# Two transformer blocks on one core: the modulations' closing products come one chunk later

## The chip, the cores and the metric

The kernel runs on one NeuronCore of a Trainium2 chip, as one launch. The metric is device microseconds (us) for the whole launch, lower is better. The engines are named as the profile names them: PE is TensorE's products, PEld its weight loads, DVE is VectorE, ACT ScalarE, POOL GpSimd, and SP is SyncE, whose queue issues nearly all transfers.

## What is computed

Two blocks of two layers each act on 512 tokens of width 1024. In the first block each layer mixes by sliding-window attention, retention and gated linear attention; in the second a layer has attention and a gated feed-forward part, and there is a second stream of 256 context tokens. Every layer is modulated: a vector `c` (one for the tokens, one more for the context) is multiplied by a large weight matrix, and the result is split into shifts, scales and gates.

```
mod = c_act @ w_mod + b_mod                                # 1024 x 3072 in block 1, 1024 x 6144 in block 2
shift, scale, gate = jnp.split(mod[:, None, :], 3, axis=-1)
h = rms_norm(x, pre_gain) * (1.0 + scale) + shift
...
return x + gate * rms_norm(y, post_gain)
```

These matrix-vector products are what the change is about. They don't depend on the tokens, so that they can be made at any time before their layer needs them.

## The kernel before

The work is written as Python generators which are woven into one another; a scheduler then fixes one order of instructions for each engine, and each engine runs its own in that order. Nearly all matrix work is in `dense` (line 427): 1024 x 128 weights arrive by a transfer into a tile `wr`, ACT rounds them to `wh` (line 422), POOL or DVE makes the rest `wl` (lines 398, 400), and PE adds 24 products into a PSUM bank: 16 with `wh`, 8 with `wl`. PSUM has eight banks; the kernel uses two under the name `b`, two under `d`, and two pairs under `s`. Everything short goes through the two banks `b`: scores of the linear attention, transposes, sums of squares, and the modulations.

The modulations are a background stream: `mods` (line 729) is a generator, and `tick` (line 360) advances it at a given rate while a stage is woven. It is started with lists of groups: once in layer 0 of block 1 (three calls of `mods` in a chain: 4, 12 and 8 chunks), once in layer 1 of block 1 (4 chunks), once from the context stage on (12), and once in the feed-forward part of block 2's first layer (24). A chunk is 256 columns of the weights and goes like this:

- Two transfers (line 738) bring the 1024 x 256 weights as two tiles `mr`, out of three buffers.
- `mod_sum` (line 708) makes 8 products `b<-mr,mc`. The vectors `mc` are only 32 columns wide, so that four products, for four quarters of the rows, stand in four strips of 32 partitions of one bank `b`; the other four add to them. In the trace each product is two instructions.
- `mod_cols` (line 719) copies that bank on ACT into a tile `ms` (line 723), and two small products with the constant `mod_sel` (`b<-mod_sel,ms`) add the four strips and turn the result into columns, in another tile of the name `b`.
- DVE adds the bias and writes the columns where they are wanted (line 744).

In the start of the kernel (line 634 on) four larger chunks are made in the same way by the same two functions, without the background. Which of the two banks a `b` tile gets is the scheduler's choice.

Of the kernel before, what the change touches and what calls it, by code (L numbers as in the profile page):

```python
# [11 lines left out]
F32 = mybir.dt.float32  # L12
# [11 lines left out]
KD = D // 128  # L24
# [102 lines left out]
def _consts():  # L127
# [5 lines left out]
    for l in range(7):  # L133
        s = 1 << l
        qt = (i // s) % 2 == 1
        start = (i // s) * s
        w[:, l] = np.where(qt, (j >= start) & (j <= i), (j > i) & (j < start + s))
        masks[:, l] = (j // (2 * s) == i // (2 * s)) & ((j // s) % 2 == 0) & ((i // s) % 2 == 1)
# [61 lines left out]
class Net:  # L200
# [187 lines left out]
    def mm(self, out, lhsT, rhs, start, stop):  # L388
        self.nc.tensor.matmul(out, lhsT, rhs, start=start, stop=stop)  # L389
# [244 lines left out]
    def start(self):  # L634

        nc, I = self.nc, self.I
        with self.phase("start") as ph:
            x = ph.tile([128, KD, S], F32, name=self.name("x"))
            for i in range(8):
                w = slice(KD // 8 * i, KD // 8 * (i + 1))  # L640
                nc.sync.dma_start(x[:, w], I["x"][:, w])
            self.setup()
            outs, b, vecs = self.mod1[0]
            m = outs[0]
            r = self.rstd(self.square_sums([x[:, k, :] for k in range(KD)], S), S)
            gain = self.common.tile([128, KD], F32, name="gain_start")
            h = self.new_h(S)
            acc = [self.bank([128, S], "d") for _ in range(2)]
            for _ in range(2):
                w = self.wide()  # L650
                acc += [w[:, 0, :], w[:, 1, :]]
            ws = []
            units = 0, 1, 11, 12, 13, 14
            for c in range(4):
                pieces = []
                for p in range(4):
                    raw = self.tl(ph, [128, 2, 512], F32, "raw", 6)
                    nc.sync.dma_start(raw, I["w_mod_start"][c, :, 2 * p:2 * p + 2, :])
                    pieces.append(raw)
                ps = self.mod_cols(self.mod_sum(pieces, vecs, range(4)), ph)  # L660
                for i, g in enumerate((1, 0)):
                    w = slice(g * KD + 2 * c, g * KD + 2 * c + 2)
                    nc.vector.tensor_add(m[:, w], ps[:, 2 * i:2 * i + 2, 0], b[:, w])
                if c < 3:
                    for u in units[2 * c:2 * c + 2]:
                        src = I["w_in"][0, u].rearrange("p k c -> p (k c)")
                        ws.append(self.weights(src, 1024, (ph, f"u{u}") if u else None))
                ks = slice(2 * c, 2 * c + 2)
                nc.vector.scalar_tensor_tensor(gain[:, ks], m[:, KD + 2 * c:KD + 2 * c + 2], 1.0, self.pre[:, 0, ks],
                                               op0=ALU.add, op1=ALU.mult)  # L670
                for k in (2 * c, 2 * c + 1):
                    self.norm_tile(h, x, k, S, r, gain, m[:, 0:KD])
                if c:
                    self.outer(ws[:2 * c], h, acc, range(2 * c, 2 * c + 2))
                if c < 3:
                    self.outer(ws[2 * c:], h, acc[2 * c:], range(2 * c + 2))
            with self.ahead(-50):
                self.angles()
        return h, dict(zip(units, acc))
# [36 lines left out]
            self.mm(ps[j:j + 32, :], c[:, k, :], pieces[k // per][:, k % per, :], x < 4, x >= 4)  # L716
        return ps

    def mod_cols(self, ps, pool):

        n = ps.shape[1]
        t = self.tl(pool, [128, n], F32, "ms", 1)
        self.nc.scalar.copy(t, ps)
        o = self.bank([128, n // 128, 2])
        for f in range(n // 128):
            self.mm(o[:, f, :], t[:, f * 128:f * 128 + 128], self.mod_sel, f == 0, f == n // 128 - 1)
        return o

    def mods(self, m, wsrc, groups):
        nc = self.nc  # L730
        outs, b, vecs = m
        for g in groups:
            for q in range(4):
                pieces = []
                for p in range(2):
                    raw = self.tl(self.mp, [128, 4, 256], F32, "mr", 3)
                    yield
                    nc.sync.dma_start(raw, wsrc[4 * g + q, :, 4 * p:4 * p + 4, :])
                    pieces.append(raw)
                o = self.mod_cols(self.mod_sum(pieces, vecs, (1, 0)), self.mp)  # L740
                w = slice(g * KD + 2 * q, g * KD + 2 * q + 2)
                for i, (_, n) in enumerate(vecs):
                    if g < n:
                        nc.vector.tensor_add(outs[i][:, w], o[:, :, i], b[:, w])

    def gain1(self, gain, scale, name):

# [1208 lines left out]
```

## Time and profile before

| | us |
|---|---|
| median of 3 runs | 2879.4 |
| lowest, highest | 2874.68, 2889.54 |
| the profiled execution | 2882.13 |
| its span, from the first to the last instruction | 2880.3 |
| PE busy in it | 2473.7 |
| DVE, ACT, POOL busy | 1267.5, 1187.0, 1077.7 |

The profile is of one execution; its span leaves out 1.8 us that lie around the first and the last instruction. An engine's idle time is put down to the engine or transfer whose signal came last before it went on. The mean clock that TensorE was granted is 0.91 of its full speed.

### The profile page before, as it was taken

To read this page: it belongs to the slowest core of one execution; us is meant where nothing else is said; L and a number is where in the kernel's file an instruction comes from. 1 tells how busy PE (TensorE), PEld (TensorE's weight loads), DVE (VectorE), ACT (ScalarE), POOL (GpSimd) and SP (SyncE) were. 2 spreads that over 40 slices of the span, in tenths; PEclk is the share of its full clock that TensorE was granted. 3 is DMA by queue.
4 is the path that set the end of the run, shared out by engine and by line. 5 is a ranking of instruction groups with operands and counts; after the bars stand their busy time and mean duration, and the time that the engine had idled before them with its cause. 6 is when DMAs were issued, how large, how long until landed. Compare 5 with 4: busy or idle time off the path is not lost. (4 is left out here: it accounts for less than half of the span.)

```text
span 2880.3 us, 35460 instructions
## 1 busy us (share of the span) xinstructions
PE 2473.7 (86%) x13052; PEld 2008.7 (70%) x13052; DVE 1267.5 (44%) x2065; ACT 1187.0 (41%) x2227; POOL 1077.7 (37%) x754
## 2 busy tenths in 40 slices
PE   6887888677979987669999899999878969799997
PEld 4765566566657765548998777777766757588886
DVE  3645356335646644356453631222635647421212
ACT  2533355333537534346554422222434536333222
POOL 2434325334623551123455632323541221433334
PEclk9988889788989987779999999999888979899999
DMA  7454544435344553335653544453442254333332
GB/s 239 131 189 143 182 132 160 139 111 169 108 128 138 188 188 119 117 107 139 178 161 136 172 145 162 146 183 115 160 135 96 86 159 114 113 110 97 101 95 74
DMA packets 170817, 400.58 MB, mean 139 GB/s; under 512 B 19378, under 2 KB 60820, under 8 KB 167316
## 3 DMA queue, kind: packets, MB, share of 16 engines
q1 hardware_dynamic: 170644, 398.31, 42.6%
q8 instruction: 104, 1.70, 0.2%
q14 instruction: 69, 0.57, 0.1%
HBM read 339.85 MB, written 58.39 MB: 138 GB/s over the span
## 5 line engine op out<-in xcount | busy, mean ns | idle before, releaser
L398 POOL TENSOR_TENSOR wl<-wr,wh 128x1024 fp32r<-128x1024 f32 (+3 forms) x245 | 537.0, 2193 | 890.8 <-ACT wh L422 435.5
L422 ACT CAST wh<-wr 128x1024 fp32r<-128x1024 f32 (+3 forms) x367 | 353.4, 963 | 745.8 <-PE d L389 290.1
L389 PE MATMUL d<-hh,wh 128*128 128x512 f32 x960 | 405.6, 422 | 20.3 <-ACT hh L556 7.8
L389 PE MATMUL d<-hl,wh 128*128 128x512 f32 x960 | 399.1, 416 | 3.3 <-POOL hl L398 1.4
L389 PE MATMUL d<-hh,wl 128*128 128x512 f32 x960 | 261.8, 402 | 0.0
L400 DVE SCALAR_TENSOR_TENSOR wl<-wr,wh 128x1024 fp32r<-128x1024 f32 (+3 forms) x122 | 151.5, 1242 | 226.5 <-PE d L389 96.3
L389 PEld LDWEIGHTS d<-hh,wh 128*128 128x128 f32 x960 | 192.4, 200 | 72.1 <-issue 12.1
L389 PEld LDWEIGHTS d<-hl,wh 128*128 128x128 f32 x960 | 192.0, 200 | 45.9 <-issue 4.9
L389 PEld LDWEIGHTS d<-hh,wl 128*128 128x128 f32 x960 | 184.7, 194 | 40.6 <-issue 2.5
L921 POOL TENSOR_TENSOR oy<-pg,pg 64x256 f32<-64x256 f32 (+1 forms) x72 | 57.4, 797 | 299.9 <-DVE pg L919 95.6
L400 DVE SCALAR_TENSOR_TENSOR pg<-b,pg 128x512 fp32r<-128x512 f32 (+1 forms) x208 | 137.3, 666 | 67.7 <-ACT pg L404 66.1
L389 PE MATMUL b<-hh,wh 128*128 128x512 f32 x416 | 165.2, 397 | 0.0
L389 PE MATMUL b<-hl,wh 128*128 128x512 f32 x416 | 164.0, 394 | 0.0
L404 ACT CAST pg<-b 128x512 fp32r<-128x512 f32 (+1 forms) x208 | 117.3, 571 | 88.9 <-PE b L896 83.4
L869 DVE TENSOR_REDUCE sm<-s 128x1 f32<-128x768 f32 (+3 forms) x144 | 121.1, 847 | 65.0 <-PE s L389 64.2
L389 PE MATMUL d<-hc,wh 128*128 128x256 f32 x656 | 104.4, 309 | 24.9 <-DVE rp L400 12.5
L937 DVE SCALAR_TENSOR_TENSOR rp<-rp,d 128x512 f32<-128x512 f32 (+1 forms) x77 | 46.8, 607 | 165.0 <-ACT rp L936 164.9
L389 PE MATMUL d<-hid,wh 128*128 128x512 f32 (+1 forms) x528 | 117.6, 365 | 1.9 <-POOL hid L398 1.5
L1725 DVE SCALAR_TENSOR_TENSOR rp<-rp,b 128x512 f32<-128x512 f32 (+1 forms) x64 | 38.1, 595 | 175.8 <-PE b L389 175.3
L389 PEld LDWEIGHTS d<-hc,wh 128*128 128x128 f32 x656 | 94.0, 209 | 30.2 <-ACT wh L422 12.1
L389 PE MATMUL b<-hid,wh 128*128 128x512 f32 (+1 forms) x528 | 110.4, 360 | 0.0
L389 PEld LDWEIGHTS d<-hid,wh 128*128 128x128 f32 x528 | 90.1, 191 | 21.2 <-issue 2.9
(412 smaller groups left out, 5191.3 us busy)
## 6 DMA issues: line engine op xcount, KB each, us to landing
wr<-in_ffn_w_in SPq DMA_DIRECT2D x132, 512.0 KB
mr<-in_ada_w SPq DMA_DIRECT2D x96, 512.0 KB
wr<-in_ffn_w_out SPq DMA_DIRECT2D x48, 512.0 KB
x<-x SPq DMA_DIRECT2D x20, 1024.0 KB
wr<-in_w_in SPq DMA_DIRECT2D x38, 512.0 KB
mr<-in_w_mod SPq DMA_DIRECT2D x32, 512.0 KB
wr<-in_ev_w_in SPq DMA_DIRECT2D x20, 512.0 KB
wr<-in_ffn_w_out SPq DMA_DIRECT2D x24, 384.0 KB
```

Source lines behind the costliest of these rows:

```text
L389: self.nc.tensor.matmul(out, lhsT, rhs, start=start, stop=stop)
L398: self.nc.gpsimd.tensor_sub(out, src, hi)
L400: self.nc.vector.scalar_tensor_tensor(out, src, scale, hi, op0=ALU.mult, op1=ALU.subtract)
L404: self.nc.scalar.copy(hi, src)
L422: nc.scalar.copy(hi[:, :n], raw[:, :n])
L869: nc.vector.reduce_max(c, s, axis=AX.X, negate=True)
L921: nc.gpsimd.tensor_tensor(d, sel(t), sel(rs), op=ALU.mult)
L937: nc.vector.scalar_tensor_tensor(t, t, 1.0, ps, op0=ALU.add, op1=ALU.mult)
L1725: nc.vector.scalar_tensor_tensor(g, g, 0.5, pu, op0=ALU.mult, op1=ALU.mult)
```

## The change

`mod_cols` is taken apart: `mod_take` copies the bank on ACT into `ms`, and `mod_cols` makes the small products from a copy. In the start the two follow each other as before. In `mods`, a chunk now makes its sums and its copy, and then the small products and the bias additions of the chunk before; `ms` has two buffers instead of one. A call's first chunk has no small products behind it, and its last chunk's come after one more `yield`, a step of the background later.

```diff
--- before.py
+++ after.py
@@ -657,7 +657,7 @@
                     raw = self.tl(ph, [128, 2, 512], F32, "raw", 6)
                     nc.sync.dma_start(raw, I["w_mod_start"][c, :, 2 * p:2 * p + 2, :])
                     pieces.append(raw)
-                ps = self.mod_cols(self.mod_sum(pieces, vecs, range(4)), ph)
+                ps = self.mod_cols(self.mod_take(self.mod_sum(pieces, vecs, range(4)), ph, 1))
                 for i, g in enumerate((1, 0)):
                     w = slice(g * KD + 2 * c, g * KD + 2 * c + 2)
                     nc.vector.tensor_add(m[:, w], ps[:, 2 * i:2 * i + 2, 0], b[:, w])
@@ -716,11 +716,14 @@
             self.mm(ps[j:j + 32, :], c[:, k, :], pieces[k // per][:, k % per, :], x < 4, x >= 4)
         return ps
 
-    def mod_cols(self, ps, pool):
-
-        n = ps.shape[1]
-        t = self.tl(pool, [128, n], F32, "ms", 1)
+    def mod_take(self, ps, pool, bufs):
+        t = self.tl(pool, [128, ps.shape[1]], F32, "ms", bufs)
         self.nc.scalar.copy(t, ps)
+        return t
+
+    def mod_cols(self, t):
+
+        n = t.shape[1]
         o = self.bank([128, n // 128, 2])
         for f in range(n // 128):
             self.mm(o[:, f, :], t[:, f * 128:f * 128 + 128], self.mod_sel, f == 0, f == n // 128 - 1)
@@ -729,6 +732,15 @@
     def mods(self, m, wsrc, groups):
         nc = self.nc
         outs, b, vecs = m
+
+        def finish(t, g, q):
+            o = self.mod_cols(t)
+            w = slice(g * KD + 2 * q, g * KD + 2 * q + 2)
+            for i, (_, n) in enumerate(vecs):
+                if g < n:
+                    nc.vector.tensor_add(outs[i][:, w], o[:, :, i], b[:, w])
+
+        last = None
         for g in groups:
             for q in range(4):
                 pieces = []
@@ -737,11 +749,12 @@
                     yield
                     nc.sync.dma_start(raw, wsrc[4 * g + q, :, 4 * p:4 * p + 4, :])
                     pieces.append(raw)
-                o = self.mod_cols(self.mod_sum(pieces, vecs, (1, 0)), self.mp)
-                w = slice(g * KD + 2 * q, g * KD + 2 * q + 2)
-                for i, (_, n) in enumerate(vecs):
-                    if g < n:
-                        nc.vector.tensor_add(outs[i][:, w], o[:, :, i], b[:, w])
+                t = self.mod_take(self.mod_sum(pieces, vecs, (1, 0)), self.mp, 2)
+                if last is not None:
+                    finish(*last)
+                last = t, g, q
+        yield
+        finish(*last)
 
     def gain1(self, gain, scale, name):
```

The scheduler makes a new order from this. Three places of PE's order follow; in the names, `mr` are the modulation weights, `mc` the vectors, `hh` and `hl` the two parts of the activations, `qb` and `pg` the operands of the linear attention.

Layer 1 of block 1, the first of its four chunks; before:

```order
L389 MATMUL d_5315<-hh_4171,wh_5311 128x512
L389 MATMUL b_5288<-mr_5106,mc_529 32x256 x4
L389 MATMUL b_5288<-mr_4979,mc_529 32x256 x4
L389 MATMUL d_5315<-hl_4172,wh_5311 128x512
L389 MATMUL d_5315<-hh_4171,wh_5311 128x512
L389 MATMUL d_5315<-hl_4172,wh_5311 128x512
L389 MATMUL b_5299<-mod_sel,ms_5297 128x2 x2
L389 MATMUL d_5315<-hh_4171,wh_5311 128x512
```

The same place now, and then the second chunk:

```order
L389 MATMUL d_5310<-hh_4171,wh_5306 128x512
L389 MATMUL b_5288<-mr_5106,mc_529 32x256 x4
L389 MATMUL b_5288<-mr_4979,mc_529 32x256 x4
L389 MATMUL d_5310<-hl_4172,wh_5306 128x512
L389 MATMUL d_5310<-hh_4171,wh_5306 128x512
L389 MATMUL d_5310<-hl_4172,wh_5306 128x512
```

```order
L389 MATMUL b_5437<-mr_5376,mc_529 32x256 x4
L389 MATMUL b_5437<-mr_5299,mc_529 32x256 x4
L389 MATMUL b_5431<-qb_1077_4845,pg_5354 128x512
L389 MATMUL d_5460<-hh_4171,wh_5456 128x512
L389 MATMUL d_5460<-hl_4172,wh_5456 128x512
L389 MATMUL b_5448<-mod_sel,ms_5297 128x2 x2
L389 MATMUL d_5460<-hh_4171,wh_5456 128x512
```

The first chunk's small products are gone from behind its sums; they stand in the second chunk (`ms_5297` is the first chunk's copy), again some products behind its sums.

Latent projections and windowed attention of block 2, the last chunk but one; before:

```order
L498 MATMUL b_10559<-ident,sm_10340 128x128 x2
L389 MATMUL d_10500<-pg_10551,ev_9910 128x512
L389 MATMUL b_10569<-mr_10297,mc_529 32x256 x4
L389 MATMUL b_10569<-mr_10033,mc_529 32x256 x4
L389 MATMUL b_10580<-mod_sel,ms_10578 128x2
L896 MATMUL b_10587<-ident,ep_10463 128x128
L896 MATMUL b_10587<-ident,ep_10473 128x128
L896 MATMUL b_10587<-ident,ep_10483 128x128
L896 MATMUL b_10587<-ident,ep_10493 128x128
L389 MATMUL b_10580<-mod_sel,ms_10578 128x2
L896 MATMUL b_10598<-ident,ep_10463 128x128
```

Now:

```order
L498 MATMUL b_10554<-ident,sm_10335 128x128 x2
L389 MATMUL d_10495<-pg_10546,ev_9905 128x512
L389 MATMUL b_10564<-mr_10292,mc_529 32x256 x4
L389 MATMUL b_10564<-mr_10028,mc_529 32x256 x4
L389 MATMUL b_10575<-mod_sel,ms_10021 128x2 x2
L909 MATMUL b_10582<-ident,ep_10458 128x128
L909 MATMUL b_10582<-ident,ep_10468 128x128
L909 MATMUL b_10582<-ident,ep_10478 128x128
L909 MATMUL b_10582<-ident,ep_10488 128x128
L909 MATMUL b_10593<-ident,ep_10458 128x128
```

The transposes of `ep` stand behind the small products as before; these are now of the chunk before (`ms_10021`), and both of them stand ahead of the transposes.

The feed-forward part of block 2, one of 24 chunks; before:

```order
L389 MATMUL b_15061<-hh_14290,wl_15058 128x512 x8
L389 MATMUL b_15095<-mr_15093,mc_529 32x256 x4
L389 MATMUL b_15095<-mr_15023,mc_529 32x256 x4
L389 MATMUL d_15118<-hh_14290,wh_15114 128x512
L389 MATMUL d_15118<-hl_14291,wh_15114 128x512
L389 MATMUL d_15118<-hh_14290,wh_15114 128x512
L389 MATMUL d_15118<-hl_14291,wh_15114 128x512
L389 MATMUL b_15106<-mod_sel,ms_15104 128x2 x2
L389 MATMUL d_15118<-hh_14290,wh_15114 128x512
```

Now:

```order
L389 MATMUL b_15056<-hh_14290,wl_15053 128x512 x8
L389 MATMUL b_15090<-mr_15088,mc_529 32x256 x4
L389 MATMUL b_15090<-mr_15018,mc_529 32x256 x4
L389 MATMUL b_15101<-mod_sel,ms_15011 128x2 x2
L389 MATMUL d_15113<-hh_14290,wh_15109 128x512
L389 MATMUL d_15113<-hl_14291,wh_15109 128x512
```

The small products have moved from behind four products of the next unit to the place right behind the sums, and read the copy of an earlier chunk. In SP's order some transfers of `mr` have changed places with transfers near them; the first such change is behind the weights `wr` that line 417 issues at 159.56 us of the trace.

## Rows read from the trace of the kernel before

**Rows 1.** Page, part 1: busy time, share of the span, instructions of each engine.
```profile
PE 2473.7 (86%) x13052; PEld 2008.7 (70%) x13052; DVE 1267.5 (44%) x2065; ACT 1187.0 (41%) x2227; POOL 1077.7 (37%) x754
```

**Rows 2.** TensorE's waits (total us, times, longest): whole run, then 0 to 130 us.
```profile
PE b L389 <- ACT ms L723: 36.8, 15, 15.8
...
PE b L389 <- ACT ms L723: 2.1, 3, 0.7
```

**Rows 3.** Timeline, 128 to 150 us: start, length, engine, line, operation [idle before <-releaser].
```profile
141.62 0.36 ACT L723 COPY ms<-b 128x256 f32<-128x256 f32 x1
...
142.04 1.01 PE L389 MATMUL b<-mod_sel,ms 128*128 128x2 f32 x4 [3.83 <-ACT ms L723]
```

**Rows 4.** Timeline, 148 to 172 us, SyncE, ScalarE and TensorE.
```profile
159.56 10.38 SPq L417 DMA_DIRECT2D wr<-in_w_in  x4
...
166.11 1.04 ACT L422 CAST wh<-wr 128x1024 fp32r<-128x1024 f32 x1 [11.74 <-DMA wr<-in_w_in]
...
167.21 0.50 PE L389 MATMUL d<-hh,wh 128*128 128x512 f32 x1 [3.88 <-ACT wh L422]
```

**Rows 5.** Timeline, 189 to 226 us, TensorE, SyncE and VectorE.
```profile
204.70 1.07 PE L389 MATMUL b<-mr,mc 128*32 128x256 f32 x16 [0.96 <-DVE oy L1122]
...
206.02 4.08 SPq L738 DMA_DIRECT2D mr<-in_w_mod  x2
...
208.23 0.73 DVE L1122 COPY_PREDICATED oy<-gla_mask,b 128x512 f32<-128x512 uint8 x1
...
208.79 0.88 PE L389 MATMUL b<-mod_sel,ms 128*128 128x2 f32 x4 [2.13 <-ACT ms L723]
...
219.10 1.88 PE L389 MATMUL b<-mr,mc 128*32 128x256 f32 x16 [2.47 <-DMA mr<-in_w_mod]
```

**Rows 6.** Timeline, 664 to 700 us, TensorE, ScalarE and VectorE.
```profile
666.87 0.39 PE L389 MATMUL d<-hl,wh 128*128 128x512 f32 x1
...
670.76 1.04 ACT L422 CAST wh<-wr 128x1024 fp32r<-128x1024 f32 x1 [7.20 <-DMA wr<-in_w_in]
...
674.52 1.01 PE L389 MATMUL b<-mod_sel,ms 128*128 128x2 f32 x4 [7.26 <-ACT ms L723]
...
675.40 0.77 PE L389 MATMUL d<-hh,wh 128*128 128x512 f32 x1
...
675.97 0.63 PE L389 MATMUL d<-hl,wh 128*128 128x512 f32 x1
...
676.16 0.87 DVE L400 SCALAR_TENSOR_TENSOR qb<-pg,qb 32x256 fp32r<-32x256 f32 x2
...
676.40 0.63 PE L389 MATMUL d<-hh,wh 128*128 128x512 f32 x1
...
682.23 1.56 PE L389 MATMUL b<-qb,pg 128*128 128x512 f32 x6
```

**Rows 7.** Timeline, 1250 to 1285 us, ScalarE and TensorE.
```profile
1267.98 0.42 ACT L503 ACTIVATE rp<-xc 128x256 f32<-128x256 f32 x1 [4.92 <-DMA eqnm<-rp]
...
1269.02 0.58 ACT L918 COPY pg<-b 64x512 f32<-64x512 f32 x1
...
1269.92 0.59 PE L389 MATMUL b<-mod_sel,ms 128*128 128x2 f32 x2 [15.83 <-ACT ms L723]
...
1270.37 1.09 PE L896 MATMUL b<-ident,ep 128*128 128x128 f32 x4
```

**Rows 8.** Timeline, 1720 to 1750 us, TensorE and its weight loads (PEld).
```profile
1723.13 1.07 PE L389 MATMUL b<-mr,mc 128*32 128x256 f32 x16
...
1724.13 0.19 PEld L389 LDWEIGHTS d<-hh,wh 128*128 128x128 f32 x1 [0.41 <-issue]
...
1724.47 0.40 PE L389 MATMUL d<-hl,wh 128*128 128x512 f32 x1
...
1724.71 0.40 PE L389 MATMUL d<-hh,wh 128*128 128x512 f32 x1
...
1725.18 0.50 PE L389 MATMUL b<-mod_sel,ms 128*128 128x2 f32 x4
```

## The prediction

> **What bounds the kernel now.** I read the page's busy times first: TensorE is busy 2473.7 us, 86% of the span, and no other engine is above 44% [rows 1]. So a gain has to come out of TensorE's idle time, some 406.6 us (2880.3 − 2473.7), or out of products that cost less. The change touches one kind of idle time, the small products' wait for ScalarE's copy `ms`, and the waits by releaser show how much that is: 36.8 us in 15 waits, of which 2.1 us in 3 belong to the start, whose order stays [rows 2]. That leaves 34.7 us in 12 waits, 1.2% of the time: no gain out of this wait can be larger.
>
> Then I looked those 12 up in the timeline. Four are long: 3.83 us at 142 [rows 3], 2.13 at 209 [rows 5], 7.26 at 675 [rows 6] and 15.83 at 1270 [rows 7]. The first three are first chunks of a call of `mods`, which lose the small products behind their sums. The other eight share 34.7 − 29.05 = 5.65 us. In the feed-forward part, with 24 of the 64 chunks, the small products start without a wait [rows 8]. For each long wait the question is what TensorE meets next: a wait that goes is worth only what the next one doesn't take back.
>
> **The change, part by part.** The count of products, copies, additions and transfers stays; what moves is the place of the small products, and with it some transfers in SP's order. I work against the profiled execution, 2882.13 us, 2.7 above the median of 2879.4.
>
> *The wait at 142, 3.83 us.* ScalarE casts the weights `wh` at 166.11 after 11.74 us of waiting for a transfer `wr` that SP issued at 159.56, and TensorE's product behind that waits 3.88 us and starts at 167.21 [rows 4]. SP's order is the old one up to that issue, so the transfer comes no earlier, and TensorE would wait 3.8 us more at 167 in place of 142. I take 0; the ends are 0 and −3.8.
>
> *The wait at 209, 2.13 us.* The next stop is at 219.10, 2.47 us for a transfer `mr` [rows 5]. Its issue at 206.02 needs a buffer that the sums at 204.70 set free, not the small products; so it lands as before and takes the gain back. I take 0 (0 to −2.1).
>
> *The wait at 675, 7.26 us.* Here the late part starts in earnest: the products behind it are `d<-hh,wh` and its kin, whose cast ended at 671.8 (670.76 + 1.04), long before [rows 6]. So the stall as such goes. Two things decide what is left. Behind the stall, products follow each other at 0.43 us (676.40 − 675.97), against 0.24 in the feed-forward part (1724.71 − 1724.47) [rows 6, 8]; 20 of them fill 675.40 to 682.23, that is 0.34 each, and at 0.24 they would take 4.8 in place of 6.8, 2.0 us less. With this, the upper end is 7.3 + 2.0 = 9.3. But the next user, `b<-qb,pg` at 682.23, needs the splits `qb`, which VectorE finishes at 677.03 (676.16 + 0.87) whatever TensorE does, since ScalarE ahead of them was held by the transfer `wr` for 7.20 us [rows 6]. So that product can come forward by at most 682.23 − 677.03 = 5.2. I take −5, the nearer bound (0 to −9.3).
>
> *The wait at 1270, 15.83 us.* This is the largest and the one that I don't count. ScalarE reaches the copy late because it waits 4.92 us for the transfer `eqnm`, until 1267.98, and ends its copy out of a `b` bank only at 1269.60 (1269.02 + 0.58) [rows 7]. In the new order the small products read an old copy, but they and the transposes `b<-ident,ep` behind them need two `b` banks: one is that which ScalarE empties at 1269.60, the other holds the new sums until the held copy is made. So the name of the wait changes, from the copy to a bank, and its end moves from 1269.92 to about 1269.6. I take −0.3 (0 to −15.8).
>
> *The eight small waits, 5.65 us.* The two `b` banks decide here too: where the small products' bank is the one that this chunk's own sums have filled, they still wait for the same copy. I take about a third, −2 (0 to −5.7).
>
> *The seam in the feed-forward part.* After the sums, the first product lies 0.34 us ahead of the next (1724.47 − 1724.13), an ordinary one 0.24, so that the seam costs 0.10 [rows 8]. Before, the small products made a second break in the run of `d`; now they stand at the seam, and 24 × 0.10 = 2.4 us can go at most. I take the half, −1.2 (0 to −2.4).
>
> By the Trainium skill, page "TensorE: Matmul & The Clock Gate", Part 2 ("What happens when you issue a matmul"), TensorE pulls weight loads ahead of products that still run. The row speaks against it at this place: the weight load behind the sums stands idle for 0.41 us with nothing to wait for [rows 8]. By the rule the seam would vanish with the change, and this term would be −2.4.
>
> *What it adds.* One more step of the background per call of `mods` costs no engine time. A second `ms` buffer costs 1 KB per partition. The swapped places in SP's queue, from 160 us on through layer 0: a transfer put behind a pair of `mr` comes up to 4.08 us later [rows 5], the `mr` as much earlier. I take 0 with ends −4 and +4, since both kinds were waited for at some place [rows 4, 5].
>
> The sum: 0 + 0 − 5 − 0.3 − 2 − 1.2 = −8.5. From 2882.13 this gives 2873.6 for a profiled execution and 2870.9 for the median; I say **2871**. With the terms' ends around it, without the 15.83, this case reaches from 2862 to 2879.
>
> **The rivals.**
>
> *More comes back (2860).* The gaps at 142 and 209 aren't taken back, since a unit ahead in time pulls later issues forward, and the clock behind 675 recovers: −3.8 − 2.1 − 9.3 − 2 − 2.4 = −19.6. For it: every releaser behind those waits is a chain through the other engines, and SP's issues follow buffers that TensorE sets free. Against it: both transfers were issued by events that the change leaves in place [rows 4, 5].
>
> *Nothing comes back (2879).* The −5 at 675 and the rest are taken by the next transfer or the next user of a bank. For it: ScalarE itself sits 7.20 us in wait of `wr` there [rows 6], so the stretch may go at the pace of the transfers; and TensorE's small waits are all for two banks. Against it: the products right behind the stall had their operands ready. The Trainium skill, same page, section "HAM oscillation — how this bites in real kernels", reports that double-buffered PSUM results gave a kernel that already ran well no further gain (126.6 to 125.5 us); by that this case would be the likeliest, and only rows of the feed-forward part, where nothing waits [rows 8], agree with it so far.
>
> *Slower (2896): the late product waits for a bank's reader on VectorE.* Before, the small products came after their own copy, some products behind the sums. Now they can stand right behind the sums, where the other `b` bank may still be under its reader. The nearest case: sums ending at 205.77 (204.70 + 1.07), and the copy with mask on VectorE, which reads a `b` bank behind the splits, ending at 208.96 (208.23 + 0.73) [rows 5]: 3.2 us, with all of TensorE's queue behind it. The 24 chunks of layer 0 stand beside such work; if 8 of them pay it, that is 25.5 − 8.5 = 17 us more. It decides from a reader that ends over 1.07 us behind the start of the sums, and from 8 chunks on it outweighs 14.4 + 8.5. For it: the sums themselves wait 0.96 us for this reader [rows 5]. Against it: in the new order, too, several products stand between sums and small products at nearly all places of that stretch.
>
> **How the numbers follow.** The forecast has 0.49, more coming back 0.21, nothing 0.21, slower 0.09. The range, 2856 to 2888, takes in the forecast's own, the first two rivals with 4 us below the first for part of the 15.83, and 9 above the second for a few bank waits or swapped transfers; outside are the third rival and most of a full return of the 15.83. About 0.5%, 14.4 us, is what a measurement of this kernel can tell from no change: faster means below 2865.0, slower above 2893.8. Faster: the first rival and 0.02 of the forecast's lower end, 0.23. Slower: the third, 0.09. Within: 0.68.
>
> **What the profile of the changed kernel would show.** Right: TensorE's wait for `ms` falls from 36.8 us to under 8; the gap near 675 is gone and `b<-qb,pg` behind it comes some 5 us earlier against its neighbours; near 167 the wait for `wh` grows to about 7.7, near 219 that for `mr` to about 4.6; near 1270 a wait of some 15 us stays, now put down to a bank's reader on ScalarE; in the feed-forward part TensorE stays busy throughout, with a pitch per chunk shorter by 0.05. Wrong: if the 15.83 us at 1270 vanish without a wait of that size within the next 50 us; if `b<-mod_sel,ms` or the sums wait for VectorE in layer 0 for over 10 us in all; or if the feed-forward stretch moves by over 3 us, which no term here allows.

## The result: 1.1% faster, more than the range allowed

| | us |
|---|---|
| before, median of 4 runs | 2877.9 |
| changed, median of 4 runs (2843.78 to 2853.33) | 2847.62 |
| ratio, 95% interval | 0.9889 (0.9855 to 0.9924) |
| changed, 6 more runs beside 11 of before | 2849.07 against 2878.02, ratio 0.9896 (0.9875 to 0.9917) |
| the profiled execution of the changed kernel | 2850.94, span 2849.2 |

The forecast was 2871 with a range down to 2856. The change takes 30 us, 3.5 times the 8.5 that I had summed up.

TensorE's busy time on the page and its waits over the whole run now read:

```profile
PE 2467.3 (87%) x13052; PEld 2004.1 (70%) x13052; DVE 1262.4 (44%) x2065; ACT 1187.1 (42%) x2227; POOL 1079.5 (38%) x754
```

```profile
PE b L389 <- DVE oy L1135: 19.0, 10, 4.2
...
PE d L389 <- ACT wh L422: 17.7, 4, 6.3
...
PE b L389 <- ACT pg L931: 16.4, 2, 16.0
...
PE b L389 <- DMA mr<-in_w_mod: 7.1, 3, 3.8
...
PE b L389 <- ACT ms L721: 4.5, 5, 1.6
```

The wait for `ms` has fallen from 36.8 to 4.5 us [rows 2], as was meant. A reader could stop here and call that the gain. The other rows forbid it: 16.0 us stand under another name now, the wait for a cast `wh` and that for VectorE's `oy` have grown. So I set the same products of both traces (the n-th of a name) against each other and read how far the changed kernel is ahead: 0.2 us at 110, 24.7 at the end of layer 0 (470 to 480 us of before), 22.3 at 620, 23.9 at 770, 24.5 at 1350, 25.4 at 1640, 26.3 at 1970, 31.6 at the end. **Most of the gain is made between 130 and 460 us**, where I had expected none to stay. (The 5.3 us behind 1970, where no modulation is left, belong to that execution of before: all sixteen kernels of the next section run 1.1 to 7.7 us ahead of it from 1970 to 2270.)

Place by place, the rows that answer to those of before. At 142 the wait is gone, and the clock with it is better; TensorE in 128 to 150 us, before:

```profile
128.00:150.00 22.00, 18.17 (x82) 14.32 (x81) 12.95 (x18) 7.26 (x15) 12.90 (x13) 0.84 0.40 139
```

and changed (the first number after the 22.00 is TensorE's busy time, the third last the granted clock):

```profile
128.00:150.00 22.00, 22.00 (x108) 17.02 (x107) 15.12 (x22) 9.09 (x19) 13.78 (x14) 1.00 0.43 148
```

The next stop takes a part back, in the changed kernel's timeline at 158 to 168 us:

```profile
162.71 1.04 ACT L422 CAST wh<-wr 128x1024 fp32r<-128x1024 f32 x1 [13.84 <-DMA wr<-in_w_in]
...
163.81 0.80 PE L389 MATMUL d<-hh,wh 128*128 128x512 f32 x1 [5.98 <-ACT wh L422]
```

5.98 in place of 3.88 us [rows 4]. The transfer is not where it was, though: the cast starts at 162.71, not 166.11.

Around 675 the stall is gone and three others stand there, in the changed kernel at 640 to 700 us:

```profile
652.04 2.79 PE L389 MATMUL b<-qb,pg 128*128 128x512 f32 x6 [2.54 <-DVE oy L1135]
...
659.06 1.86 PE L389 MATMUL b<-rq,rk 128*128 128x512 f32 x4 [4.23 <-DVE oy L1135]
...
665.08 0.47 PE L389 MATMUL d<-pg,rv 128*128 128x512 f32 x1 [2.37 <-DMA rv<-rv]
```

The product `b<-qb,pg` of 682.23 [rows 6] now starts at 652.04, 30.2 us earlier and so 7.9 ahead of its neighbours' 22.3; by 700 all but 1.6 of that is gone.

At 1270 the wait has only changed its name, in the changed kernel at 1222 to 1250 us:

```profile
1242.05 0.42 ACT L503 ACTIVATE rp<-xc 128x256 f32<-128x256 f32 x1 [4.96 <-DMA eqnm<-rp]
...
1243.10 0.58 ACT L931 COPY pg<-b 64x512 f32<-64x512 f32 x1
...
1243.73 1.01 PE L389 MATMUL b<-mod_sel,ms 128*128 128x2 f32 x4 [16.02 <-ACT pg L931]
```

The same squares, the same transfer, the same reader of a `b` bank as in [rows 7], and 16.02 us in place of 15.83. In the feed-forward part a chunk of the changed kernel reads:

```profile
1697.11 1.07 PE L389 MATMUL b<-mr,mc 128*32 128x256 f32 x16
1698.11 0.61 PE L389 MATMUL b<-mod_sel,ms 128*128 128x2 f32 x4
1698.58 0.48 PE L389 MATMUL d<-hh,wh 128*128 128x512 f32 x1
1698.89 0.40 PE L389 MATMUL d<-hl,wh 128*128 128x512 f32 x1
```

From the start of the sums to the second product behind them that is 1.78 us with the small products inside. Before, the same piece took 1.34 (1724.47 − 1723.13), and the small products with the next product 0.45 more than a plain product's 0.23 [rows 8]: 1.79. There is next to nothing in it.

### The profile page after: what moved, and what is told of

It reads as the page before. It is cut to its first block, busy times and chain, and to the rows that moved or that the text cites. A ratio compares the mean times of both kernels' runs of the same rounds, so it can differ in the third digit from the quotient of the medians.

```text
span 2849.2 us, 35397 instructions
## 1 busy us (share of the span) xinstructions
PE 2467.3 (87%) x13052; PEld 2004.1 (70%) x13052; DVE 1262.4 (44%) x2065; ACT 1187.1 (42%) x2227; POOL 1079.5 (38%) x754
## 5 line engine op out<-in xcount | busy, mean ns | idle before, releaser
L389 PE MATMUL d<-hh,wh 128*128 128x512 f32 x960 | 399.1, 416 | 19.3 <-ACT hh L556 7.8
L389 PE MATMUL b<-hh,wl 128*128 128x512 f32 x416 | 104.0, 390 | 0.0
```

## Experiments

e1 to e8 and e12 to e15 keep the changed kernel's code and switch its two parts call by call (e9 to e11 are the kernel before with one line more, e16 is the changed kernel): `late` (the small products come a chunk late) and `tail` (the extra step at a call's end).

```diff
-    def mods(self, m, wsrc, groups):
+    def mods(self, m, wsrc, groups, late=True, tail=True, bufs=2):
...
+                if not late:
+                    finish(t, g, q)
+                    continue
                 if last is not None:
                     finish(*last)
                 last = t, g, q
-        yield
-        finish(*last)
+        if tail:
+            yield
+        if last is not None:
+            finish(*last)
```

With both off in all calls, every engine's order is that of the kernel before. The table gives all runs; "fetch 3" and "fetch 4" are the starts of the first transfer `rk` of the retention's third and fourth head in layer 0, "held" the time that SP waited ahead of fetch 3 (from 225 us on) by the profile's waits put down to a transfer `mr`, blank where its longest such wait was under 3.5 us, "end" the start of the first `b<-blk,rp` behind 420 us, just after layer 0's windowed attention. These four are from one profiled execution each; executions differ by up to 3 us from the start on.

| kernel | median | ratio, 95% interval | fetch 3 | held | fetch 4 | end |
|---|---|---|---|---|---|---|
| before | 2878 to 2880 | | 259.3 | 8.4 | 313.9 | 460.3 |
| changed | 2847.6 | 0.9889 (0.9855 to 0.9924) | 243.9 | | 295.2 | 434.6 |
| e1 late and step, layer 0 only | 2853.5 | 0.9899 (0.9883 to 0.9915) | 243.9 | | 296.2 | 437.5 |
| e2 all but layer 0 | 2871.3 | 0.9966 (0.9951 to 0.9980) | 259.0 | 8.3 | 312.6 | 457.4 |
| e3 step alone | 2866.8 | 0.9943 (0.9926 to 0.9961) | 243.1 | | 302.7 | 438.4 |
| e4 late, first call, no step | 2881.0 | 1.0000 (0.9987 to 1.0013) | 252.6 | 8.4 | 307.4 | 454.1 |
| e5 late, no step | 2875.1 | 0.9982 (0.9968 to 0.9996) | 256.2 | 8.4 | 310.4 | 450.2 |
| e6 before, rate 0.73 | 2865.4 | 0.9953 (0.9939 to 0.9968) | 247.7 | | 299.0 | 438.9 |
| e7 before, rate 0.79 | 2865.2 | 0.9952 (0.9937 to 0.9968) | 252.8 | | 303.9 | 445.7 |
| e8 changed, rate 0.70 | 2858.1 | 0.9930 (0.9909 to 0.9951) | 243.5 | | 300.2 | 438.1 |
| e9 pause at the fifth chunk | 2869.5 | 0.9962 (0.9947 to 0.9978) | 244.6 | | 295.9 | 441.7 |
| e10 pause at the sixth chunk | 2876.3 | 0.9986 (0.9972 to 1.0000) | 253.0 | 8.3 | 300.0 | 444.9 |
| e11 pause at the ninth chunk | 2879.8 | 1.0003 (0.9988 to 1.0018) | 258.8 | 8.3 | 313.1 | 451.7 |
| e12 late and step in layer 0, rate 0.79 | 2874.2 | 0.9990 (0.9982 to 0.9999) | 243.0 | | 310.3 | 448.5 |
| e13 step, late in calls 1 and 3 | 2859.2 | 0.9938 (0.9916 to 0.9961) | 246.4 | | 306.5 | 436.1 |
| e14 step, late in call 2 | 2861.1 | 0.9935 (0.9912 to 0.9957) | 241.7 | | 292.7 | 429.5 |
| e15 step alone, late in the other 40 | 2859.9 | 0.9928 (0.9908 to 0.9948) | 240.5 | | 302.8 | 436.9 |
| e16 changed, again | 2849.1 | 0.9896 (0.9875 to 0.9917) | 242.7 | | 295.1 | 430.2 |

Below, gains are differences of medians to before in the same rounds (2879.8 for e1 to e4, 2877.9 for e5 to e12, 2878.0 for e13 to e16).

**Which stretch, which part.** e1 has `late=False, tail=False` in the three calls outside layer 0, e2 in the three calls of layer 0; e3 has `late=False` in layer 0 (the step stays) and the others off; e4 is late in the first call only, without the step:

```diff
-self.mods(m1[0], I["w_mod"][0], (2,))
+self.mods(m1[0], I["w_mod"][0], (2,), tail=False)
```

> Late only in the 24 chunks of layer 0 of block 1; the other 40 chunks as before. The engines' orders are those of the changed kernel up to the end of layer 0 and those of the kernel before behind it. In the traces the same products of both kernels lie 21 to 23 us apart at the end of that stretch. Theory A (the gain is made in layer 0 and kept): 22 to 26 us less than before. Theory B (my prediction's picture: layer 0 takes its own gains back, the sum comes from the later places): 0 to 5 us less.

> The complement: the 24 chunks of layer 0 as before, late in the other 40. Theory A: 3 to 8 us less than before (some 1.5 near 675, a little in the feed-forward part). Theory B: the larger part of the 30 us, 20 or more. If the two parts don't interact, the gains of this run and of the one with layer 0 alone add up to that of the change.

> Nothing is late; only the one more step of the background at the end of each of the three calls in layer 0 is kept (and the second copy buffer). It moves later chunks and with them 586 rows of TensorE's order and the places of some transfers. Theory C (the gain of layer 0 comes from the order that the scheduler happened to make): 12 to 25 us less than before. Theory D (it comes from the small products that no longer wait for the copy): within 4 us of before.

> Late only in the first call of mods (4 chunks, from 130 to about 190 us), without the extra step, so that only 36 rows of TensorE's order differ from before and 6 of SP's. It takes away the wait of 3.83 us at 142 alone. My prediction: 0 (the transfer behind it takes it back). Theory D: 3 to 6 us less, since in the changed kernel TensorE's clock there is 1.00 in place of 0.84 and the weights behind it land 3.4 us earlier. Theory C: 0 to 3 us less.

Layer 0 alone is worth 26.3, the rest 8.5; together that is 34.8, some 5 more than the change itself, which the intervals allow. Theory A holds: most of the gain is made in layer 0. But e3, in which nothing is late, already has 13.0 of it, and its TensorE still waits 38.8 us in all for `ms`. And e4, without the 3.83 us at 142, is the kernel before to within 0.13% (3.7 us): its profile shows the same clock of 1.00 there and then 6.52 us of waiting for `wh`. So about half of what pays in layer 0 is not what the change is about; the extra step moves the background, and with it the order.

**Late without the step, and the order moved by other means.** e5 has `tail=False` in layer 0 and the rest off; e6 and e7 are the kernel before with another rate, e8 the changed kernel with another rate:

```diff
-                                       self.mods(ada[0], I["ada_w"][0], (1, 0))), 0.76)
+                                       self.mods(ada[0], I["ada_w"][0], (1, 0))), 0.73)
```

> Late in the 24 chunks of layer 0, but without the extra step at the end of the three calls (there the last chunk's small products come at once). Theory H (the gain of layer 0 comes through SP's queue: a transfer mr whose buffer is still in use holds up the fetches rq, rk, rv of the retention behind it; what counts is how many mr stand ahead of the third and fourth fetch): here these are 20 and 29 of 48, as in the kernel before (19 and 28 in the changed one and with the step alone), so 0 to 6 us less than before. Theory D (the small products that no longer wait): 15 to 26 us less.

> The kernel before with one number changed: the background of layer 0 advances at 0.73 in place of 0.76 per step. Nothing is late and nothing else moves by hand. 19 and 28 mr stand ahead of the third and fourth retention fetch. Theory H: 10 to 20 us less than before, as with the step alone. Theory D: within 4 us of before.

> The kernel before with the rate 0.79: 21 and 30 mr stand ahead of these fetches, one more than before. Theory H: 5 to 20 us more than before. Theory D: within 4 us of before. If both this and the run with 0.73 are faster, the order of before was simply an unlucky one among many.

> The changed kernel in full with the rate 0.70: 17 and 25 mr ahead of these fetches. Theory H: 5 to 15 us less than the changed kernel (35 to 45 less than before), as long as the chunks that are left at the end of the layer find room beside the windowed attention. Theory D: the same as the changed kernel, 30 less than before.

Theory D falls with e5: 2.8 us by medians, 1 to 9 by the interval, with 21 of layer 0's 24 chunks late. Theory H in its first form, a count of `mr` ahead of the fetches, falls with e7: one more `mr` ahead, and yet 12.7 us faster; the changed kernel with 0.70 was some 10 us slower than with 0.76, where 5 to 15 less were expected. What holds is that the order counts: 0.73 and 0.79 are both 12 to 13 us faster than 0.76 with nothing else changed. The kernel before had an order that its neighbours don't have.

**What is bad in that order.** The traces show one place. SP's queue in the kernel before, 225 to 262 us:

```profile
238.97 3.82 SPq L803 DMA_DIRECT2D aq<-rp  x4
242.89 2.48 SPq L738 DMA_DIRECT2D mr<-in_w_mod  x2
245.41 0.75 SPq L417 DMA_DIRECT2D wr<-in_w_in  x1
255.79 0.33 SPq L738 DMA_DIRECT2D mr<-in_w_mod  x1
258.95 0.33 SPq L806 DMA_DIRECT2D rq<-rq  x1
259.33 2.42 SPq L806 DMA_DIRECT2D rk<-rk  x4
```

and what SP waited for, 238 to 262 us:

```profile
SPq L738 <- DMA mr<-in_w_mod: 8.4, 1, 8.4
SPq L803 <- ACT rp L406: 8.3, 1, 8.3
SPq L806 <- PE b L389: 3.1, 1, 3.1
```

Two `mr` go out late, at 242.89, because the `aq` store ahead of them waited for ScalarE. TensorE's next sums wait for the first of them; the second line is the retention's last product `b<-rq,rk` of the head before:

```profile
254.66 1.94 PE L389 MATMUL b<-mr,mc 128*32 128x256 f32 x16 [7.52 <-DMA mr<-in_w_mod]
...
258.25 0.67 PE L389 MATMUL b<-rq,rk 128*128 128x128 f32 x2
```

The 20th `mr` needs the buffer that these sums free, so that SP stands until 255.79; and behind it in the queue stand `rq`, `rk` and `rv` of the retention's third head. They don't need the `mr`, but they weren't free to go either: `rq` goes out at 258.95, right behind the end of that `b<-rq,rk` (258.25 + 0.67 = 258.92), and SP waits for it (the third line of its waits). This product stands behind the held sums in TensorE's order. So two things hold the fetch, SP's queue and TensorE's own wait of 7.52 us ahead of this product, and the wait that ends last is the one for the product.

SP has that wait of 8.3 or 8.4 us in the traces of before, e2, e4 and e5, and at most 2.8 us in those of e1, e3, e6, e7, e8 and the changed kernel, all at least 12 us faster than before. That an `mr` without a buffer holds SP is not peculiar to the slower kernels, though: the same stand is put down to TensorE's sums elsewhere, in the changed kernel at 225 to 262 us:

```profile
SPq L750 <- PE b L389: 9.3, 3, 7.0
```

To test the place, one empty step was put into the second call of the kernel before, ahead of its fifth, sixth or ninth chunk:

```diff
             for q in range(4):
                 pieces = []
+                if (g, q) == pause:
+                    yield
                 for p in range(2):
...
-self.mods(m1[1], I["w_mod"][1], (1, 0, 2))
+self.mods(m1[1], I["w_mod"][1], (1, 0, 2), pause=(0, 0))
```

(e10 has `(0, 1)`, e11 `(2, 0)`.) e12 is e1 at the rate 0.79.

> The kernel before with one empty step in the second call of layer 0, ahead of its fifth chunk; nothing late. The orders are those of before up to some 240 us; from there SP fetches the retention's third head (rq, rk, rv) ahead of the 20th transfer mr, which in the trace of before waits for its buffer until 255.79 and so holds the fetch until 259. Over nine kernels the stretch of layer 0 ends the later, the later this fetch is (259: 460 us, 256: 450, 253: 446, 248 and 243: 438). Theory F (this fetch behind that mr is the place): 10 to 16 us less than before, as with the step alone. Theory G (the loss lies further on, from 270 us): the same as the next run. Theory D: within 4 us of before.

> The same empty step one chunk later: the 20th mr stands ahead of the third fetch again, and only 94 rows of TensorE's order and 8 of SP's differ from the run with the step ahead of the fifth chunk; what comes behind the fetch is rearranged in both. Theory F: within 5 us of before, 7 or more behind the other run. Theory G: 10 to 16 us less than before in both.

> The same empty step three chunks later still, so that the orders are those of before up to some 320 us, the fourth fetch of the retention (314 us, behind 29 mr) included. Theories F and G with the loss ahead of 320 us: within 4 us of before. If it is 10 us faster, the loss lies in the windowed attention behind it.

> The kernel before at rate 0.79 with the 24 chunks of layer 0 late, extra steps included: the partner of the run with 0.79 that had nothing late (2865, 12.7 less than before). Theory D2 (on an order that isn't held up, late products are worth as much again: layer 0 late against the step alone was 2853.5 against 2866.8): 2850 to 2857. Theory O (a late product is worth 0 to 5 us; the rest of that difference is again the order): 2858 to 2870.

Theory F holds in kind: 8.4, 1.6 and −1.9 us. e9 and e10 differ in 94 rows of TensorE's order and 8 of SP's, and by 6.8 us, with 3 to 11 by the scatter of their 7 and 12 runs. (The two profiled executions don't show that difference: 2869.65 and 2868.75 us.) SP's queue in e9, 225 to 262 us, with the fetch ahead of the 20th `mr`:

```profile
236.83 3.80 SPq L805 DMA_DIRECT2D aq<-rp  x4
240.73 2.48 SPq L740 DMA_DIRECT2D mr<-in_w_mod  x2
244.21 0.33 SPq L808 DMA_DIRECT2D rq<-rq  x1
244.59 4.02 SPq L808 DMA_DIRECT2D rk<-rk  x4
...
254.01 1.62 SPq L417 DMA_DIRECT2D wr<-in_w_in  x2
256.48 0.80 SPq L740 DMA_DIRECT2D mr<-in_w_mod  x2
```

and in e10, behind it:

```profile
236.56 2.50 SPq L740 DMA_DIRECT2D mr<-in_w_mod  x2
239.11 0.72 SPq L417 DMA_DIRECT2D wr<-in_w_in  x1
249.45 0.33 SPq L740 DMA_DIRECT2D mr<-in_w_mod  x1
252.60 0.33 SPq L808 DMA_DIRECT2D rq<-rq  x1
252.98 2.42 SPq L808 DMA_DIRECT2D rk<-rk  x4
```

In e9 the fetch issues 3.5 us behind the last pair of `mr` (244.21 − 240.73), in e10 16.0 us (252.60 − 236.56). In both it goes right behind the end of the same `b<-rq,rk`, and TensorE's order has changed around it as well. e9, TensorE:

```profile
243.74 0.44 PE L389 MATMUL b<-rq,rk 128*128 128x128 f32 x2
...
255.78 1.07 PE L389 MATMUL b<-mr,mc 128*32 128x256 f32 x16 [2.50 <-DVE oy L1124]
```

Here the product stands ahead of the sums. In e10 it starts at 251.90, behind sums that start at 248.31 after 7.54 us of waiting for `mr`. TensorE's waits for `mr` between 230 and 300 us (total, times, longest), e9:

```profile
PE b L389 <- DMA mr<-in_w_mod: 1.3, 2, 0.7
```

e10:

```profile
PE b L389 <- DMA mr<-in_w_mod: 9.2, 2, 7.5
```

The size came out smaller than the 10 to 16 expected; e3, e6 and e7, with 12 to 13, change more places than this one. So e9 against e10 shows that this place is worth some 7 us. It doesn't show which of the two waits costs them, SP's in its queue or TensorE's for the `mr`, since both go at once; that SP's queue is the cause is argued only.

Two other runs speak for TensorE's wait. e7 fetches as late as e10 (252.8 and 253.0), but TensorE waits 1.8 us at most for `mr` there between 225 and 315 us, and it is 12.7 us faster than before. e12 has an early third fetch (243.0), is slower than both theories had it, and 9.0 us slower (2874.2 against 2865.2) than e7, the kernel at the same rate with nothing late. In it the sums at 251.13 wait 7.53 us for `mr`, as in the kernels that are held; its TensorE between 225 and 315 us:

```profile
PE b L389 <- DMA mr<-in_w_mod: 11.1, 2, 7.5
```

Against it stands e8, where a wait of 7.43 us at 251.47 doesn't make the stretch end late. e12's fourth fetch is also as late as that of e5 (310.3); no run takes these waits apart. Over all 18 traces the end of the stretch goes with the two fetches (correlation 0.85 with either, each counted, like the end, from the first `b<-qb,pg`), which doesn't make them its cause.

**What late products are worth on an order that isn't held up.** e13 and e14 keep the steps of layer 0 and are late in calls 1 and 3, and in call 2; e15 is e3 with the other 40 chunks late; e16 is the changed kernel.

> The extra steps in layer 0 as with the step alone, and late in the first and third call (12 of the 24 chunks), which leaves SP's order as it was with the step alone but for 6 rows. Theory O (the time follows the order, a late product is worth 0 to 3 us in all): 2862 to 2868, as the step alone (2866.8). Theory D2 (late products are worth another 13 us on a good order, so half of that for half of the chunks): 2856 to 2862.

> The extra steps in layer 0, and late only in the second call (12 chunks). SP's order is now that of the run with all of layer 0 late but for 6 rows; the third fetch of the retention stands two weight transfers further ahead than with the step alone. Theory O: 2851 to 2857, as all of layer 0 late (2853.5). Theory D2: 2856 to 2862.

> Layer 0 with the extra steps but nothing late, the other 40 chunks late. If the parts add up (13 and 8.5): 2856 to 2860, 8 to 12 behind the changed kernel.

> The changed kernel itself, in the same rounds: 2844 to 2853, as in its first four runs. If the sum of the two halves of the change (26.3 with layer 0, 8.5 with the rest) holds: 2842 to 2848.

e15 adds up within the noise: 18.2 us, against 13.0 + 8.5, and 10.8 behind e16. e16 itself, 2849.1, lies a little above what the sum of the halves would give. e13 and e14 lie in the ranges of Theory D2, but their intervals reach into those of O. They gain 18.8 and 16.9 by medians, so that each half of the late chunks is worth some 4 to 6 us beside the step's 13.0; by the ratios it is 1.4 and 2.3 (0.05% and 0.08% of 2878), within the intervals of nothing. Together with the step's 13 this gives 17 to 23, while e1 with all of it has 26.3, so **3 to 10 us stay open**. I can't put them to the order or to the lateness: in the two profiled executions e1 and e3 end layer 0 within 1 us of each other, and e1 gains 13 us behind it, where both have the same order, in steps of up to 1.8 us, several of them at waits for transfers (that for `rk` near 782 us is 4.60 in e3 and 2.78 in e1). The mean granted clock goes the same way (0.917 over e1's four runs, 0.914 over e3's six, 0.910 over the 23 of before); whether as cause or as effect of the waits wasn't tried.

No version beat the changed kernel.

## Why the prediction was wrong

- **The bound of 34.7 us** was read right and used wrongly. It bounds what waits for `ms` can give. The time could come from elsewhere too, and did.
- **The step that failed: "The swapped places in SP's queue ... I take 0 with ends −4 and +4".** I saw that transfers changed places from 160 us on, priced one place by the 4.08 us of a pair's issue, and stopped there. What a place is worth depends on who waits in it: in the order of before, sums that TensorE meets ahead of their late `mr` hold it for 7.5 us, an `mr` without a buffer holds SP's queue for 8.4 us, and the retention's third fetch waits behind both. e9 against e10 puts this place at some 7 us, e3 the extra step as a whole, which moves TensorE's order too, at 13 (11 to 21 by the interval). Of layer 0's 26.3 us, 3 to 10 stay without a cause. "One more step of the background per call costs no engine time" is true, and was the costliest sentence of the text. The pattern stood in [rows 5] even: TensorE waits 2.47 us for an `mr` that SP could not issue earlier.
- **142 us: 0.** Right by e4 (0 ± 3.7), though not by the working: the transfer did come 3.4 us earlier, and what is won there is lost behind it.
- **209 us: 0.** A wait for `mr` is there as forecast, at 215.74 and 2.79 us long (I said 4.6); alone it wasn't tried.
- **675 us: −5.** The bound by VectorE's splits was wrong, the product came 7.9 earlier and not 5.2 at most; then 2.54, 4.23 and 2.37 us of new waits took most of it. The traces put what stays at 1.6 to 3.2: between 620 and 880 us the five kernels that are late in layer 1 fall back by 0.4 us on the average against before, the twelve others by 3.7.
- **1270 us: −0.3.** Right: 16.02 us, under the name of the bank's reader on ScalarE.
- **Small waits, −2.** Between 880 and 1370 us the late ones gain 1.5 us and the others fall back by 2.0, which is 3.5 us in favour of the late ones; with 675 us and the feed-forward part that is some 7.5 us, near my −5 −0.3 −1.2 and part of the −2, and near the 8.5 (6 to 14) of e2.
- **Feed-forward seam, −1.2.** Too much: 0.9 us between 1640 and 1970 in the profiled pair, 0.01 us per chunk by the rows above. By the rule of the Trainium skill that I had weighed there ("TensorE: Matmul & The Clock Gate", Part 2), 2.4 us should have gone; the rows agree with it as little as with mine.
- **The range.** "With the terms' ends around it ... from 2862 to 2879" is not what the ends add up to: they reach from 2851.8 (27.6 less than 2879.4) to 2883.4. The measured 2847.62 lies outside that as well.
- **The rivals.** "More comes back" came nearest (2860), for another reason. The third rival's sign shows: waits for VectorE's `oy` grew from 9.5 us to 19.0, but were outweighed.
- **What would prove it wrong** named 10 us of such waits in layer 0 and the 15.83 us vanishing. Neither happened (6.8 us there), so that the list had no line for the place where it failed.

## What to carry to other kernels

Where a change makes a scheduler write a new order, the new order is a change of its own: run it without the intended part (here one empty step, or a rate of 0.73) before the gain is put down to the idea. And read a single-queue issuer like an engine: ask of each issue that waits for a buffer what stands behind it, and what that would set free. Then ask the same of the engine that would free the buffer. In e9 the background's transfer went behind the foreground's fetch, and its products behind the product that the fetch waits for; that both moves are needed isn't shown.

## What was not expected of the hardware

- SP's queue stands still behind an issue that waits for its buffer: in the kernel before it issued nothing from 246.16 to 255.79 us. The fetch behind it would not have gone at 246 either, since the product that it waits for ended at 258.92.
- The clock paid locally and not in the end: without the 3.83 us of idle time TensorE was granted 1.00 in place of 0.84 from 128 to 150 us (e3, which keeps the wait, has 0.84 as well), and e4, which has the 1.00 too, was not faster (ratio 1.0000).
- One number of ±0.03 in the rate of a background stream moved the whole kernel by 12 to 13 us, nearly half of what the change itself gave.
